# A 4096 x 4096 x 4096 matmul with GELU on one core: A transposed by VectorE from a staged layout, and another opening

## The chip, the cores and the metric

The kernel runs on one core of a Trainium2 chip. The time is the device time of one execution in microseconds (us). A kernel's time is the median of its runs. Beside the times there is one profiled execution with its trace; its span runs from the first to the last recorded instruction.

Names used below: TensorE (PE; its weight loads are PEld), VectorE (DVE), ScalarE (ACT), GpSimd (POOL) and SyncE (SP) are the engines. SBUF is the on-chip memory, PSUM the accumulators of TensorE (eight banks). A load is a DMA that an engine's queue issues; GpSimd's queue issues the loads here, since they convert float32 to bfloat16 on the way, and SyncE's queue issues the stores.

## The reference

```
def setup_inputs():
    m, k, n = 4096, 4096, 4096
    return {
        "a": np.random.randn(m, k).astype(np.float32),
        "b": np.random.randn(k, n).astype(np.float32),
    }

def reference(a: np.ndarray, b: np.ndarray) -> np.ndarray:
    x = np.matmul(a, b)
    return 0.5 * x * (1 + np.tanh(np.sqrt(2 / np.pi) * (x + 0.044715 * x**3)))
```

TensorE multiplies a 128 x 128 piece of A, held with K on the partitions (so A has to be transposed), by a 128 x 512 piece of B, also with K on the partitions. A 128 x 512 result tile sums 32 such matmuls in one PSUM bank. The whole product is 8192 matmuls.

## The kernel before

The rows of A are taken in four blocks of 1024 (`mb`). A block holds eight row tiles of 128 (`ms`), kept transposed in `aT` (one buffer for the whole kernel). For each block all eight chunks of 512 columns of B (`nci`) are loaded as `Bc` (128 x 32 x 512, 4 MB as bfloat16; two buffers), each with one load on GpSimd's queue (L88). For each chunk and row tile, 32 matmuls (L97) run over all of K into one PSUM bank `acc` (four banks). I call the 8 x 32 = 256 matmuls of one chunk in one block a pass.

A is transposed by TensorE. `emit_build` loads a row tile in two halves (L65, 128 partitions x 8 KB of float32 each, stage `a16`, eight buffers), transposes it in 128 x 128 pieces into PSUM (`tp`, L73, two banks), and ScalarE copies four pieces at a time into `aT` (L81). The first block's builds stand in the first pass, before each row tile's matmuls; the build of the next block's row tile stands in a block's last pass, behind the row tile's matmuls.

The result tile goes from PSUM to SBUF (ScalarE, L105), three VectorE instructions compute x(1 + 0.044715 x^2) (L107, L108, L116), ScalarE applies a sigmoid (L117), VectorE multiplies by x (L119), and SyncE's queue stores the tile (L120).

The order of the instructions on each engine is not simply the order of the code. The framework's scheduler hands out the buffers of each pool, puts the instructions of each engine in an order, and adds the waits on semaphores; an instruction whose buffer is free can come ahead of one that stands earlier in the code.

Of the kernel before, what the change touches and what calls it, by code (L numbers as in the profile page):

```python
# [2 lines left out]

# [5 lines left out]

F32 = mybir.dt.float32  # L10
BF16 = mybir.dt.bfloat16
ACT = mybir.ActivationFunctionType
ALU = mybir.AluOpType

GELU_C = 0.044715
SIG_SCALE = 2.0 * math.sqrt(2.0 / math.pi)


@with_exitstack
def kernel(  # L20
    ctx: ExitStack,
    tc: tile.TileContext,
    a: bass.AP,
    b: bass.AP,
    out: bass.AP,
):
    nc = tc.nc
    P = nc.NUM_PARTITIONS

    M, K = a.shape  # L30
    K2, N = b.shape
    assert K == K2
    assert M % P == 0 and K % P == 0 and N % P == 0

    MB = min(1024, M)
    assert M % MB == 0
    NMB = M // MB
    MS_PER = MB // P
    NC = min(512, N)
    assert N % NC == 0  # L40
    NCH = N // NC
    NKT = K // P
    KSTAGE = min(K, 2048)
    assert K % KSTAGE == 0 and KSTAGE % P == 0
    KT_PER_STAGE = KSTAGE // P
    TPG = min(4, KT_PER_STAGE)
    assert KT_PER_STAGE % TPG == 0

    const_pool = ctx.enter_context(tc.tile_pool(name="const", bufs=1))
    at_pool = ctx.enter_context(tc.tile_pool(name="at", bufs=1))  # L50
    astage_pool = ctx.enter_context(tc.tile_pool(name="astage", bufs=8))
    bc_pool = ctx.enter_context(tc.tile_pool(name="bc", bufs=2))
    ev_pool = ctx.enter_context(tc.tile_pool(name="ev", bufs=3))
    psum_pool = ctx.enter_context(tc.tile_pool(name="psum", bufs=4, space=bass.MemoryType.PSUM))

    ident = const_pool.tile([P, P], BF16, name="ident")
    make_identity(nc, ident[:])

    aT = at_pool.tile([P, NKT, MB], BF16, name="aT")

    def emit_build(mb: int, ms: int):
        row0 = mb * MB + ms * P
        for kh in range(K // KSTAGE):
            a16 = astage_pool.tile([P, KSTAGE], BF16, name="a16", tag="a16")
            nc.gpsimd.dma_start(  # L65
                out=a16[:, :],
                in_=a[row0 : row0 + P, kh * KSTAGE : (kh + 1) * KSTAGE],
            )
            for g in range(KT_PER_STAGE // TPG):
                tp = psum_pool.tile([P, TPG * P], BF16, name="tp", tag="tp", bufs=2)  # L70
                for j in range(TPG):
                    ktl = g * TPG + j
                    nc.tensor.transpose(  # L73
                        tp[:, j * P : (j + 1) * P],
                        a16[:, ktl * P : (ktl + 1) * P],
                        ident[:, :],
                    )
                kt0 = kh * KT_PER_STAGE + g * TPG
                src = tp.rearrange("p (j q) -> p j q", j=TPG)
                dst = aT[:, kt0 : kt0 + TPG, ms * P : (ms + 1) * P]  # L80
                nc.scalar.copy(out=dst, in_=src)  # L81

    for mb in range(NMB):
        m0 = mb * MB
        for nci in range(NCH):
            n0 = nci * NC
            Bc = bc_pool.tile([P, NKT, NC], BF16, name="Bc", tag="bc")
            nc.gpsimd.dma_start(  # L88
                out=Bc[:, :, :],
                in_=b[:, n0 : n0 + NC].rearrange("(kt p) n -> p kt n", p=P),  # L90
            )
            for ms in range(MS_PER):
                if mb == 0 and nci == 0:
                    emit_build(0, ms)
                acc = psum_pool.tile([P, NC], F32, name="acc", tag="acc", bufs=4)
                for kt in range(NKT):
                    nc.tensor.matmul(  # L97
                        acc[:, :],
                        aT[:, kt, ms * P : (ms + 1) * P],
                        Bc[:, kt, :],  # L100
                        start=(kt == 0),
                        stop=(kt == NKT - 1),
                    )
                x_sb = ev_pool.tile([P, NC], F32, name="x_sb", tag="x")
                nc.scalar.activation(x_sb[:, :], acc[:, :], ACT.Copy)  # L105
                w = ev_pool.tile([P, NC], F32, name="w", tag="w")
                nc.vector.tensor_tensor(out=w[:, :], in0=x_sb[:, :], in1=x_sb[:, :], op=ALU.mult)  # L107
                nc.vector.tensor_scalar(  # L108
                    out=w[:, :],
                    in0=w[:, :],  # L110
                    scalar1=GELU_C,
                    scalar2=1.0,
                    op0=ALU.mult,
                    op1=ALU.add,
                )
                nc.vector.tensor_tensor(out=w[:, :], in0=w[:, :], in1=x_sb[:, :], op=ALU.mult)  # L116
                nc.scalar.activation(w[:, :], w[:, :], ACT.Sigmoid, scale=SIG_SCALE)  # L117
                y = ev_pool.tile([P, NC], F32, name="y", tag="y")
                nc.vector.tensor_tensor(out=y[:, :], in0=w[:, :], in1=x_sb[:, :], op=ALU.mult)  # L119
                nc.sync.dma_start(  # L120
                    out=out[m0 + ms * P : m0 + (ms + 1) * P, n0 : n0 + NC],
                    in_=y[:, :],
                )
                if nci == NCH - 1 and mb + 1 < NMB:
                    emit_build(mb + 1, ms)


# [1 line left out]
_INS = ['a', 'b']  # L129
_OUTS = [((4096, 4096), 'float32')]  # L130


# [23 lines left out]
```

## Time and profile before

| | |
|---|---|
| median of 3 runs | 1891.46 us (1891.25 to 1892.04) |
| span of the profiled execution | 1889.7 us, granted TensorE clock 1.000 |
| busy: TensorE, VectorE, ScalarE, GpSimd | 1832.4, 655.4, 446.2, 88.8 us |
| HBM read, written | 335.54 MB, 67.11 MB |
| loads on GpSimd's queue | 32 of Bc, 64 of a |
| stores on SyncE's queue | 256 |

A group row of the profile reads: line, engine, operation, output <- input, shapes, count | busy us, mean ns of one | idle time of the engine ahead of them, and what ended it. A row in order of time reads: start, duration (both us), engine, line, operation, names, count, and in brackets the idle time ahead of it with what ended it. A row of the view by stretches reads: start:end, length, busy us and count of PE, PEld, DVE, ACT and POOL, the granted clock, the mean busy share of the 16 DMA engines, and GB/s as landed. Matmuls are pipelined, so the duration of one matmul is longer than the distance from one to the next.

### The profile page before, as it was taken

What the parts mean: (1) busy time and instruction counts of PE and PEld (TensorE: products, weight loads), DVE (VectorE), ACT (ScalarE), POOL (GpSimd) and SP (SyncE); (2) the same over time, 40 slices, a digit from 0 to 9 for tenths busy, and PEclk for the clock granted to TensorE, in tenths of its full rate; (3) what the DMA queues carried; (4) which work ended last, traced back from release to release, by engine and by line L of the source; (5) the groups of instructions that cost most, each with busy time, mean ns of one, the idle gap of its engine ahead of it and who ended that gap; (6) DMA issues with size and microseconds to landing.
All of it is one profiled execution on the core that took longest, in us unless ns stands there. A gap on an engine that the chain in (4) does not pass through costs nothing.

```text
span 1889.7 us, 21528 instructions
## 1 busy us (share of the span) xinstructions
PE 1832.4 (97%) x9033; PEld 860.3 (46%) x9216; DVE 655.4 (35%) x1024; ACT 446.2 (24%) x770; POOL 88.8 (5%) x102
## 2 busy tenths in 40 slices
PE   3999999999999999999999999999999999999998
PEld 2444444444544444444554444444454444444443
DVE  0233333333233333333323333333323333333333
ACT  2521111113511111111441111111154111111111
POOL 2100000000100000000110000000000000000000
PEclk9999999999999999999999999999999999999999
DMA  9995445667876664456995666644496445666511
GB/s 191 222 183 107 97 96 120 127 128 137 175 145 128 128 117 98 94 111 129 177 173 108 122 128 128 129 98 97 98 210 117 86 94 117 128 123 129 114 54 40
DMA packets 177761, 236.29 MB, mean 125 GB/s; under 512 B 5632, under 2 KB 136704, under 8 KB 177664
## 3 DMA queue, kind: packets, MB, share of 16 engines
q0 software_dynamic: 140800, 167.78, 52.9%
q1 hardware_dynamic: 36864, 67.13, 9.9%
q8 instruction: 72, 1.18, 0.2%
q14 instruction: 25, 0.20, 0.0%
HBM read 335.54 MB, written 67.11 MB: 213 GB/s over the span
## 4 chain that ended last, share of the span: by engine, by line
PE 94%; ACT 3%; DMA 1%; issue 1%; DVE 1%; POOL 0%; ACTq 0%; POOLq 0%
PE acc L97 92%; PE tp L73 3%; ACT aT L81 1%; DMA a<-in_a_dram 1%; ACT x_sb L105 1%; DVE w L108 0%; ACT w L117 0%; DVE w L107 0%; DVE w L116 0%; POOL Bc L88 0%; ACT L117 0%; DVE y L119 0%; ACTq L105 0%; POOL ident masks.py:199 0%; POOL ident masks.py:197 0%
## 5 line engine op out<-in xcount | busy, mean ns | idle before, releaser
L97 PE MATMUL acc<-Bc,aT 128*128 128x512 bf16 x8009 | 1790.3, 379 | 9.1
L97 PEld LDWEIGHTS <-aT 128*128 128x128 bf16 x8192 | 798.2, 98 | 931.0 <-issue 0.3
L107 DVE TENSOR_TENSOR w<-x_sb 128x512 f32<-128x512 f32 x256 | 177.3, 692 | 1015.6 <-ACT x_sb L105 1015.6
L105 ACT ACTIVATE x_sb<-acc 128x512 f32<-128x512 f32 x256 | 152.9, 597 | 944.4 <-PE acc L97 915.3
L117 ACT ACTIVATE w<-w 128x512 f32<-128x512 f32 x256 | 161.1, 629 | 465.9 <-DVE w L116 465.9
L119 DVE TENSOR_TENSOR y<-w,x_sb 128x512 f32<-128x512 f32 x256 | 177.1, 692 | 198.2 <-ACT w L117 198.2
L116 DVE TENSOR_TENSOR w<-w,x_sb 128x512 f32<-128x512 f32 x256 | 177.3, 693 | 8.8
L81 ACT COPY aT<-tp 128x512 bf16<-128x512 bf16 x256 | 136.7, 586 | 28.8 <-PE tp L73 28.4
L73 PE MATMUL tp<-ident,a 128*128 128x128 bf16 x1024 | 95.0, 221 | 41.2 <-DMA a<-in_a_dram 28.3
L108 DVE TENSOR_SCALAR w<-w 128x512 f32<-128x512 f32 x256 | 123.7, 483 | 8.7
L88 POOL DMA_DIRECT2D Bc<-in_b_dram x32 | 54.0, 1687 | 1439.3 <-PE acc L97 1398.2
L73 PEld LDWEIGHTS <-a 128*128 128x128 bf16 x1024 | 76.5, 98 | 91.0 <-issue 45.6
L65 POOL DMA_DIRECT2D a<-in_a_dram x64 | 34.2, 537 | 245.6 <-PE tp L73 226.6
L81 ACT ACT_TABLE_LOAD x1 | 1.3, 1283 | 0.7 <-PEq L140 0.7
L117 ACT ACT_TABLE_LOAD x1 | 1.3, 1283 | 0.0
masks.py:199 POOL TENSOR_SCALAR_AFFINE_SELECT ident<-ident 128x128 bf16<-128x128 bf16 x1 | 0.3, 306 | 0.1
masks.py:197 POOL MEMSET ident<- 128x128 bf16 x1 | 0.2, 205 | 0.3 <-POOLq L140 0.3
L140 POOL MEMSET const-float32-0.0<- 128x1 f32 x1 | 0.1, 99 | 0.2 <-issue 0.2
L140 POOL MEMSET const-bfloat16-1.0<- 128x1 bf16 x1 | 0.1, 102 | 0.0
L140 POOL MEMSET const-uint8-127<- 128x1 uint8 x1 | 0.1, 102 | 0.0
L140 POOL MEMSET const-float32-1.0<- 128x1 f32 x1 | 0.1, 99 | 0.0
## 6 DMA issues: line engine op xcount, KB each, us to landing
Bc<-in_b_dram POOLq DMA_DIRECT2D x32, 4096.0 KB, 27.2
out_dram<-y SPq DMA_DIRECT2D x256, 256.0 KB, 3.4
a<-in_a_dram POOLq DMA_DIRECT2D x64, 512.0 KB, 17.3
```

What stands on the lines that cost most here:

```text
L65: nc.gpsimd.dma_start(out=a16[:, :], in_=a[row0 : row0 + P, kh * KSTAGE : (kh + 1) * KSTAGE],)
L73: nc.tensor.transpose(tp[:, j * P : (j + 1) * P], a16[:, ktl * P : (ktl + 1) * P], ident[:, :],)
L81: nc.scalar.copy(out=dst, in_=src)
L88: nc.gpsimd.dma_start(out=Bc[:, :, :], in_=b[:, n0 : n0 + NC].rearrange("(kt p) n -> p kt n", p=P),)
L97: nc.tensor.matmul(acc[:, :], aT[:, kt, ms * P : (ms + 1) * P], Bc[:, kt, :], start=(kt == 0), stop=(kt == NKT - 1),)
L105: nc.scalar.activation(x_sb[:, :], acc[:, :], ACT.Copy)
L107: nc.vector.tensor_tensor(out=w[:, :], in0=x_sb[:, :], in1=x_sb[:, :], op=ALU.mult)
L108: nc.vector.tensor_scalar(out=w[:, :], in0=w[:, :], scalar1=GELU_C, scalar2=1.0, op0=ALU.mult, op1=ALU.add,)
L116: nc.vector.tensor_tensor(out=w[:, :], in0=w[:, :], in1=x_sb[:, :], op=ALU.mult)
L117: nc.scalar.activation(w[:, :], w[:, :], ACT.Sigmoid, scale=SIG_SCALE)
L119: nc.vector.tensor_tensor(out=y[:, :], in0=w[:, :], in1=x_sb[:, :], op=ALU.mult)
L140: nc = _bacc.Bacc("TRN2", target_bir_lowering=False, num_devices=1)
```

## The change

- A's loads. A row tile of 128 rows is loaded in four chunks of 1024 along K, each chunk with four loads of 32 partitions. The stage `a16` holds on partition 32g + mm the 256 values of K of group g for the four rows mm, 32 + mm, 64 + mm and 96 + mm (pieces of 1 KB of float32). That makes 16 loads a row tile, 512 in all.
- The transpose. One VectorE instruction per stage transposes it in 32 x 32 blocks, reading with a step of eight elements and writing eight 128 x 128 pieces of the row tile's `aT`. TensorE's transposes, the identity and ScalarE's copies are gone. `aT` is one tile per row tile, with ten buffers.
- B's order along K. Within each 1024 of K, partition p holds rows 8p to 8p + 7, so that B's order fits A's. `Bc` has three buffers and is loaded in four parts of 1024 rows of K; the first two chunks are loaded in 16 parts each.
- The opening. Four row tiles times two chunks of B accumulate in all eight PSUM banks, with the contraction outermost: the loads come quarter by quarter of K, and all eight tiles take a quarter's matmuls before the next quarter. In the last quarter the eight tiles end one after the other.
- After it, row tiles 4 to 7 take chunks 0 and 1, then chunks 2 to 7 follow for all eight row tiles. Each later block goes through the chunks in the reverse order of the block before, and chunks that are still held are not loaded again.
- GELU is one ScalarE instruction from PSUM to the result tile (`Gelu_apprx_tanh`); VectorE's four instructions are gone.

```
-    aT = at_pool.tile([P, NKT, MB], BF16, name="aT")
-    def emit_build(mb: int, ms: int):
...
-                for j in range(TPG):
-                    ktl = g * TPG + j
-                    nc.tensor.transpose(
-                        tp[:, j * P : (j + 1) * P],
-                        a16[:, ktl * P : (ktl + 1) * P],
-                        ident[:, :],
-                    )
...
-                nc.scalar.copy(out=dst, in_=src)
+    at_pool = ctx.enter_context(tc.tile_pool(name="at", bufs=MS_PER + 2))
+    stage_pool = ctx.enter_context(tc.tile_pool(name="stage", bufs=8))
+    bc_pool = ctx.enter_context(tc.tile_pool(name="bc", bufs=3))
+    y_pool = ctx.enter_context(tc.tile_pool(name="y", bufs=4))
+    psum_pool = ctx.enter_context(tc.tile_pool(name="psum", bufs=8, space=bass.MemoryType.PSUM))
+    a_v = a.rearrange("(t mb mm) (c g r) -> t c g mm mb r", mb=4, mm=Q, g=4, r=RUN)
+    b_v = b.rearrange("(c p j) n -> c p j n", p=P, j=NJ)
+    def load_a(t, c):
+        if c == 0:
+            at[t] = at_pool.tile([P, NKT, P], BF16, name="aT", tag="aT")
+        s = stage_pool.tile([P, 4, RUN], BF16, name="a16", tag="a16")
+        for g in range(4):
+            nc.gpsimd.dma_start(out=s[g * Q : (g + 1) * Q, :, :], in_=a_v[t, c, g])
+        src = s.rearrange("p mb (q j) -> p j mb q", j=NJ)
+        dst = at[t][:, c * NJ : (c + 1) * NJ, :].rearrange("p j (mb q) -> p j mb q", mb=4)
+        nc.vector.transpose(dst, src)
...
+    def load_b(n, c, j0, j1):
+        nc.gpsimd.dma_start(
+            out=bc[n][:, c * NJ + j0 : c * NJ + j1, :],
+            in_=b_v[c, :, j0:j1, n * NC : (n + 1) * NC],
+        )
...
+    def finish(acc, t, n):
+        y = y_pool.tile([P, NC], F32, name="y", tag="y")
+        nc.scalar.activation(y[:, :], acc[:, :], ACT.Gelu_apprx_tanh)
+        nc.sync.dma_start(out=out[t * P : (t + 1) * P, n * NC : (n + 1) * NC], in_=y[:, :])
...
+    for c in range(NCHK):
+        for i in range(H):
+            load_a(i, c)
+            for n in range(2):
+                load_b(n, c, 2 * i, 2 * i + 2)
...
+    for c in range(NCHK - 1):
+        for j in range(NJ):
+            for i in range(H):
+                for n in range(2):
+                    mm(accs[i, n], i, n, c * NJ + j)
...
+    work = [(t, n) for t in range(H, MS_PER) for n in range(2)]
+    order = list(range(NCH))
+    for blk in range(MT // MS_PER):
+        for x, n in enumerate(order):
+            if blk == 0 and n < 2:
+                continue
+            work += [(blk * MS_PER + i, n) for i in range(MS_PER)]
+        order = order[::-1]
+    held = [0, 1]
...
+        if n not in held:
+            need.append(("b", n))
+            held = (held + [n])[-3:]
...
+                for c in range(NCHK):
+                    load_a(x, c)
...
+                for c in range(NCHK):
+                    load_b(x, c, 0, NJ)
+        acc = new_acc()
+        for kt in range(NKT):
+            mm(acc, t, n, kt)
+        finish(acc, t, n)
```

More of the change, by code (lines that the diff above doesn't have):

```diff
@@ L12 @@
 ACT = mybir.ActivationFunctionType
-ALU = mybir.AluOpType
-GELU_C = 0.044715
-SIG_SCALE = 2.0 * math.sqrt(2.0 / math.pi)
+P = 128
+Q = 32
+NC = 512
+KC = 1024
+NJ = KC // P
+RUN = Q * NJ
 @with_exitstack
@@ L27 @@
     nc = tc.nc
-    P = nc.NUM_PARTITIONS
     M, K = a.shape
[L31 to L40, printed above, removed]
-    NCH = N // NC
[L42 to L57, printed above, removed]
@@ L59 @@
-    aT = at_pool.tile([P, NKT, MB], BF16, name="aT")
-    def emit_build(mb: int, ms: int):
[L62 to L67, printed above, removed]
-            )
-            for g in range(KT_PER_STAGE // TPG):
-                tp = psum_pool.tile([P, TPG * P], BF16, name="tp", tag="tp", bufs=2)
-                for j in range(TPG):
-                    ktl = g * TPG + j
-                    nc.tensor.transpose(
-                        tp[:, j * P : (j + 1) * P],
-                        a16[:, ktl * P : (ktl + 1) * P],
-                        ident[:, :],
[L77 to L125, printed above, removed]
@@ new lines @@
+    _, N = b.shape
+    NCHK = K // KC
+    NKT = K // P
+    MT = M // P
+    NCH = N // NC
+    MS_PER = 8
+    H = 4
+    at_pool = ctx.enter_context(tc.tile_pool(name="at", bufs=MS_PER + 2))
[4 more added lines that the diff above has]
+    a_v = a.rearrange("(t mb mm) (c g r) -> t c g mm mb r", mb=4, mm=Q, g=4, r=RUN)
@@ new lines @@
+    b_v = b.rearrange("(c p j) n -> c p j n", p=P, j=NJ)
+    at = {}
+    bc = {}
+    def load_a(t, c):
[7 more added lines that the diff above has]
+        nc.vector.transpose(dst, src)
@@ new lines, in new_b, with mm @@
+    def new_b(n):
+        bc[n] = bc_pool.tile([P, NKT, NC], BF16, name="Bc", tag="bc")
+    def load_b(n, c, j0, j1):
[3 more added lines that the diff above has]
+        )
+    def mm(acc, t, n, kt):
+        nc.tensor.matmul(
+            acc[:, :], at[t][:, kt, :], bc[n][:, kt, :],
+            start=(kt == 0), stop=(kt == NKT - 1),
+        )
+    def finish(acc, t, n):
+        y = y_pool.tile([P, NC], F32, name="y", tag="y")
+        nc.scalar.activation(y[:, :], acc[:, :], ACT.Gelu_apprx_tanh)
+        nc.sync.dma_start(out=out[t * P : (t + 1) * P, n * NC : (n + 1) * NC], in_=y[:, :])
@@ new lines, in new_acc @@
+    def new_acc():
+        return psum_pool.tile([P, NC], F32, name="acc", tag="acc")
+    new_b(0)
+    new_b(1)
+    accs = {}
+    for c in range(NCHK):
[5 more added lines that the diff above has]
+        for n in range(2):
+            accs[i, n] = new_acc()
+    for c in range(NCHK - 1):
+        for j in range(NJ):
+            for i in range(H):
+                for n in range(2):
+                    mm(accs[i, n], i, n, c * NJ + j)
@@ new lines @@
+    c = NCHK - 1
+    for j in range(NJ - 2):
+        for i in range(H):
+            for n in range(2):
+                mm(accs[i, n], i, n, c * NJ + j)
+    for i in range(H):
+        for n in range(2):
+            for j in range(NJ - 2, NJ):
+                mm(accs[i, n], i, n, c * NJ + j)
+            finish(accs[i, n], i, n)
+    work = [(t, n) for t in range(H, MS_PER) for n in range(2)]
[6 more added lines that the diff above has]
+        order = order[::-1]
@@ new lines @@
+    held = [0, 1]
+    plan = []
+    for t, n in work:
+        need = []
+        if t not in at and ("a", t) not in plan:
+            need.append(("a", t))
+            plan.append(("a", t))
+        if n not in held:
+            need.append(("b", n))
+            held = (held + [n])[-3:]
+        yield_loads = need
+        for kind, x in yield_loads:
+            if kind == "a":
+                for c in range(NCHK):
+                    load_a(x, c)
+            else:
+                new_b(x)
+                for c in range(NCHK):
[4 more added lines that the diff above has]
+        finish(acc, t, n)
```

4 lines of the change are left out of this document (1 added, 3 removed).

## The prediction

> **What bounds the kernel now.** I read the page's busy shares, its chain and its costliest groups first, then GpSimd's queue in order of time, then the two ends of the span.
>
> ```profile
> span 1889.7 us, 21528 instructions
> PE 1832.4 (97%) x9033; PEld 860.3 (46%) x9216; DVE 655.4 (35%) x1024; ACT 446.2 (24%) x770; POOL 88.8 (5%) x102
> ...
> PE 94%; ACT 3%; DMA 1%; issue 1%; DVE 1%; POOL 0%; ACTq 0%; POOLq 0%
> ...
> L97 PE MATMUL acc<-Bc,aT 128*128 128x512 bf16 x8009 | 1790.3, 379 | 9.1
> ...
> L73 PE MATMUL tp<-ident,a 128*128 128x128 bf16 x1024 | 95.0, 221 | 41.2 <-DMA a<-in_a_dram 28.3
> ```
>
> TensorE is the chain. Its 379 ns is the length of one pipelined matmul, not its price, and 183 of 8192 records are missing, so I take the price from the spacing of the Bc loads: from the third on, each waits for the pass (256 matmuls) that frees its buffer.
>
> ```profile
> 111.78 1.69 POOL L88 DMA_DIRECT2D Bc<-in_b_dram  x1 [4.65 <-PE acc L97]
> ...
> 388.16 1.69 POOL L88 DMA_DIRECT2D Bc<-in_b_dram  x1 [53.57 <-PE acc L97]
> ...
> 573.31 1.70 POOL L88 DMA_DIRECT2D Bc<-in_b_dram  x1 [52.35 <-PE acc L97]
> ...
> 849.69 1.68 POOL L88 DMA_DIRECT2D Bc<-in_b_dram  x1 [53.56 <-PE acc L97]
> ```
>
> Between 573.31 and 849.69 lie five passes without transposes: 276.38 / 5 = 55.28 us, 215.9 ns a matmul. From 388.16 to 849.69 lies one whole block of eight passes with the next block's 256 transposes: 461.53, against 8 x 55.28 = 442.2. So a block's transposes cost 19.3 us of TensorE. The first pass ends at 111.78; without its 55.28 of matmuls the opening costs 56.5.
>
> ```profile
> 1882.80 0.60 ACT L105 ACTIVATE x_sb<-acc 128x512 f32<-128x512 f32 x1 [3.67 <-PE acc L97]
> ...
> 1886.07 0.69 DVE L119 TENSOR_TENSOR y<-w,x_sb 128x512 f32<-128x512 f32 x1 [0.76 <-ACT w L117]
> ```
>
> The matmuls end at 1882.80, the last y is ready at 1886.76, and 2.9 us of store and closing follow: a tail of 6.9. Sum: 32 x 55.28 = 1769.0, opening 56.5, three block changes 58, tail 6.9, together 1890.4 against the span of 1889.7. The median of the runs is 1891.46, so 1.8 us lie around the span.
>
> **The change part by part.**
>
> *Transposes off TensorE.* All 1024 go. Those of the three block changes were wholly in TensorE's stream: minus 58.0 (both bounds, 57 to 59, from the spacing). The first block's are counted in the opening. The matmuls stay 8192 with the same 128x512 shape and as many weight loads: 1769.0 unchanged.
>
> *The 128 VectorE transposes.* No row has one. The nearest:
>
> ```profile
> L107 DVE TENSOR_TENSOR w<-x_sb 128x512 f32<-128x512 f32 x256 | 177.3, 692 | 1015.6 <-ACT x_sb L105 1015.6
> ...
> L117 ACT ACTIVATE w<-w 128x512 f32<-128x512 f32 x256 | 161.1, 629 | 465.9 <-DVE w L116 465.9
> ...
> L108 DVE TENSOR_SCALAR w<-w 128x512 f32<-128x512 f32 x256 | 123.7, 483 | 8.7
> ```
>
> One handles 1024 elements a partition, so twice a one-input row (0.97 us) to twice a two-input row (1.38); I take 1.1, nearer the one-input form that it is. Four make a row tile, about 4.4 us of VectorE against 13.8 of TensorE for a tile's first two uses; VectorE loses its 1024 GELU instructions, so nothing else is in its way. Cost 0. The cover is gone only at four times that price. By the Trainium skill, page "Vector Engine (DVE) Microarchitecture Reference", section "The reshape front-end and per-opcode configuration", the transpose sustains one element per cycle and lane; no run here shows it yet.
>
> *GELU in one ScalarE pass.* One pass of about 0.63 us (the Sigmoid row) per 6.9 us of matmuls: hidden. At the end only, copy, four VectorE steps and Sigmoid (1882.80 to 1886.76, 3.96 us) become 0.63: minus 3.3.
>
> *DMA traffic.* B chunks are loaded 8 + 3 x 5 = 23 times instead of 32, since three stay across a reversal of the order. Bytes were hidden in the steady part already: 0. But A now comes in 512 loads of 32 partitions (128 pieces of 1 KB each) instead of 64, all on GpSimd's queue together with B.
>
> ```profile
> L88 POOL DMA_DIRECT2D Bc<-in_b_dram x32 | 54.0, 1687 | 1439.3 <-PE acc L97 1398.2
> ...
> L65 POOL DMA_DIRECT2D a<-in_a_dram x64 | 34.2, 537 | 245.6 <-PE tp L73 226.6
> ```
>
> The old A load has 128 pieces and costs 537 ns to issue; Bc with 4096 pieces costs 1687, so the price is about 0.5 plus 0.3 ns a piece. The new A load has 128 pieces again: 0.54. Sixteen make a tile, 8.6 us of queue, below 13.8 (row tiles 4 to 7, each used twice in a row). At a block change six of the eight tiles wait for buffers that come free one per 6.9 us from 48.3 us ahead of the change, and the last is needed 48.3 us behind it: 96.6 us for 6 x 8.6 = 52. Hidden.
>
> *The opening.* Before, TensorE waits for Bc and A, then transposes. After, it works as each quarter of K lands, for four row tiles and two B chunks at once, so the loads set the pace.
>
> ```profile
> 0.00:5.00 5.00, 0.00 (x0) 0.00 (x0) 0.00 (x0) 1.28 (x1) 4.03 (x10) 1.00 0.20 25
> ...
> 32.00:34.00 2.00, 2.00 (x13) 1.36 (x12) 0.00 (x0) 1.47 (x3) 0.00 (x0) 1.00 1.05 211
> ...
> 234.00:236.00 2.00, 2.00 (x11) 0.89 (x10) 0.00 (x0) 0.10 (x1) 0.00 (x0) 1.00 1.24 208
> ```
>
> The last two columns are DMA share and GB/s, in bf16 bytes as they land. At 32 only A moves (4 KB landing per packet), at 234 only B (1 KB). Time per packet is share x 16 x bytes / rate: 326 ns and 97.7 ns, a line of 21.6 ns plus 0.0743 ns a byte, so an A piece of 512 B would take 59.6 ns. One quarter holds 2048 A and 2048 B packets. By bytes alone at 208 GB/s, 3.15 MB take 15.1 us; with an A piece as dear as a B packet, 20.2; by the line and B's share of 1.24, 6.2 + 10.1 = 16.2, which I take as it is fitted to both sizes. Issuing (16 x 0.54 + 8 x 0.6 = 13.4) stays below. Full rate starts at about 4 (the first window moved 0.6 us' worth of data by 5.0, and the identity's instructions ahead are gone). The last quarter lands at 4 + 64.8 + 1 for the completion = 70, and its 64 matmuls take 13.8: done at 83.6. Less 55.3 of work, the opening costs 28.3 instead of 56.5: minus 28.2 (bounds 33 and 12).
>
> ```profile
> 29.96 0.63 PE L97 MATMUL acc<-Bc,aT 128*128 128x512 bf16 x1
> ...
> 42.30 0.38 PE L97 MATMUL acc<-Bc,aT 128*128 128x512 bf16 x1
> ...
> 46.12 0.38 PE L73 MATMUL tp<-ident,a 128*128 128x128 bf16 x4 [1.39 <-ACT aT L81]
> ```
>
> After the long first wait matmuls run slow (0.63) until about 34, with 1.00 granted in every window; after 1.39 us of idleness they are still fast. My gaps between quarters are 2.4 us, so I charge slow matmuls in the first quarter alone, where the next landing hides them. The Trainium skill, page "TensorE: Matmul & The Clock Gate", section "Part 1: The HAM clock gate", puts the fall to half speed after about 3.4 us idle: by that rule with wider gaps each later quarter would lose some 1.7 us more, an estimate, and the sum would be about 5 higher. That both gaps here fit the rule is all the trace shows.
>
> **Sum.** 1889.7 - 58.0 - 3.3 - 28.2 = 1800.2 for the span, plus 1.8 around it: 1802. What is late next is TensorE itself; only the opening and 3.6 of tail are left beside its matmuls.
>
> **The rivals.**
>
> *A chunk late at each reversal.* The three buffers of Bc then hold, say, chunks 5, 6, 7, read in the order 7, 6, 5; chunk 4 can go where 7 was, or, if buffers are handed on by age of loading, has to wait for 5's last reader. Before, both rules give the same order, so its trace can't tell. The price:
>
> ```profile
> DMA to landing us min/median/max: 24.5/27.2/38.0
> ```
>
> (of Bc). Chunk 4's last quarter would land 27.2 after the pass, its last 8 matmuls take 1.7, and 6.9 of that is work: 22.0 lost, three times 66: 1868. For it: the chunk that the code drops from its list is the one loaded first. Against it: the next rival's rows show a load going out ahead of its turn once it has a buffer, so buffers seem to be given by what is free.
>
> *B's third chunk goes ahead of A's last loads.* The queue's order is not the program's:
>
> ```profile
> 3.44 3.77 POOL L65 DMA_DIRECT2D a<-in_a_dram  x7
> 26.11 0.54 POOL L65 DMA_DIRECT2D a<-in_a_dram  x1 [18.91 <-DMA Bc<-in_b_dram]
> ...
> 35.25 1.70 POOL L88 DMA_DIRECT2D Bc<-in_b_dram  x1
> ```
>
> The second Bc went out at 35.25 with five A loads of the first block still to come, though the code puts it behind them. A whole chunk in the midst of the opening costs 4.19 MB / 208 = 20.2: 1822. Against it: there the A loads lacked buffers; here the eight stage buffers come free as fast as quarters land.
>
> *The small A loads are the bound: slower.* The ninth load, at 26.11, sat 18.91 us until the first landed, though its own buffer had never been used: eight loads are in flight, no more. If a small load takes L from issue to landing, the queue yields one per L/8. Landing times of the old A loads were:
>
> ```profile
> DMA to landing us min/median/max: 5.9/17.3/36.4
> ```
>
> At 5.9 that is 0.74 us a load, 11.8 a tile, hidden. At 1.16 us (L = 9.3) the quarters take 16 x 1.16 + 4.8 = 23.4 (plus 28 in all), tiles 4 to 7 wait 4 x 4.8 = 19, and a block change 6 x 18.6 - 96.6 = 15, times three 45: 92, which eats the gain of 89.5. Above it the change loses; at 1.25 (L = 10) plus 130 gives 1932. For it: median and maximum. Against it: these are loads of eight times the bytes, behind a 4 MB chunk. The Trainium skill, page "DMA: Bandwidth & Descriptors", section "Bandwidth", calls transfers under 64 KB dominated by descriptors and asks for 1 MiB each; section "Anatomy of one DMA" gives 2.0 us fixed each, by which 128 KB loads one at a time would be far past 1.16, and eight abreast far below. The row at 26.11 is for the latter.
>
> **How the numbers follow.** The forecast, 1802 with its own range 1793 to 1826 (15.1 to 20.2 us a quarter, slow matmuls or a late start): 0.62. B's chunk ahead, or another loss of that size (1826 to 1855): 0.12. Late chunks at reversals, 1850 to 1885: 0.17. Small loads as the bound: 0.07 slower. Gain and loss cancelling: 0.02. The range 1793 to 1870 holds the first two and over half of the third, 0.84. A measurement tells about 0.2% (4 us) from no change; so faster 0.90, same 0.03, slower 0.07.
>
> **What would show it.** Right: no TensorE transposes; passes still 55.3 us apart across block changes; the last opening matmuls near 84 with gaps of 2 to 3 us between quarters; VectorE transposes near 1.1 us; the end 3.6 us behind the last matmul. Wrong: TensorE idle some 22 us in the fourth pass of blocks 2 to 4 with Bc as releaser; idle stretches ahead of row tiles with a VectorE transpose as releaser, GpSimd waiting on A loads; the opening ending past 100.

## The result: 1800.86 us, against 1802 forecast

The changed kernel takes 1800.86 us (median of 4 runs, 1799.22 to 1802.37) beside 1891.43 of the kernel before on the same chip: a ratio of 0.9521, 95% interval 0.9507 to 0.9534. The profiled run's span is 1798.2. First the profile's page, the rows that answer to those of before (busy shares, chain, groups):

```profile
span 1798.2 us, 18458 instructions
...
PE 1765.6 (98%) x8029; PEld 801.5 (45%) x8192; DVE 248.7 (14%) x128; ACT 153.8 (9%) x257; POOL 371.5 (21%) x632
...
L74 PE MATMUL acc<-Bc,aT 128*128 128x512 bf16 x8029 | 1765.6, 379 | 29.0 <-DMA Bc<-in_b_dram 18.2
...
L62 DVE STREAM_TRANSPOSE aT<-a 128x1024 bf16<-128x1024 bf16 x128 | 248.7, 1983 | 1101.6 <-PE acc L74 965.1
L59 POOL DMA_DIRECT2D a<-in_a_dram x512 | 275.9, 553 | 452.4 <-DVE aT L62 348.1
L81 ACT ACTIVATE y<-acc 128x512 f32<-128x512 f32 x256 | 152.5, 597 | 1640.7 <-PE acc L74 1573.9
```

TensorE has matmuls only, and its whole idle time ahead of them is 29.0 us. VectorE has 128 transposes of 1.98 us, GpSimd's queue 512 loads of A at 0.553. The loads of B in order of time, and the last GELU:

```profile
524.07 3.50 POOL L68 DMA_DIRECT2D Bc<-in_b_dram  x4 [24.61 <-PE acc L74]
...
745.10 3.47 POOL L68 DMA_DIRECT2D Bc<-in_b_dram  x4 [51.80 <-PE acc L74]
...
1187.11 3.47 POOL L68 DMA_DIRECT2D Bc<-in_b_dram  x4 [51.78 <-PE acc L74]
```

```profile
1794.68 0.60 ACT L81 ACTIVATE y<-acc 128x512 f32<-128x512 f32 x1 [6.31 <-PE acc L74]
```

From 745.10 to 1187.11 is one whole block with its change: 442.01, where before it was 461.53. That is eight passes of 55.25 and nothing else. The matmuls end at 1794.68 and the span 3.5 later. So 32 x 55.25 = 1768.0, an opening of 26.7 and the tail of 3.5. Against before: block changes 3 x 19.5 = 58.6, opening 29.8, tail 3.4, together 91.8; the spans differ by 91.5.

### The profile page after: what moved, and what is told of

Its sections match the earlier page's. It is cut to its first block, busy times and chain, and to the rows that moved or that the text cites. A ratio compares the mean times of both kernels' runs of the same rounds, so it can differ in the third digit from the quotient of the medians.

```text
span 1798.2 us, 18458 instructions
## 1 busy us (share of the span) xinstructions
PE 1765.6 (98%) x8029; PEld 801.5 (45%) x8192; DVE 248.7 (14%) x128; ACT 153.8 (9%) x257; POOL 371.5 (21%) x632
## 3 DMA queue, kind: packets, MB, share of 16 engines
q8 instruction: 64, 1.05, 0.2%
## 4 chain that ended last, share of the span: by engine, by line
PE 94%; DMA 3%; POOL 2%; issue 1%; DVE 0%; ACT 0%; DVEq 0%; ACTq 0%; POOLq 0%
PE acc L74 94%; DMA Bc<-in_b_dram 2%; POOL a L59 1%; DMA a<-in_a_dram 1%; POOL Bc L68 0%; DVE aT L62 0%; ACT y L81 0%; DVEq L62 0%; ACTq L81 0%; POOLq L163 0%; POOLq L59 0%
## 5 line engine op out<-in xcount | busy, mean ns | idle before, releaser
L74 PE MATMUL acc<-Bc,aT 128*128 128x512 bf16 x8029 | 1765.6, 379 | 29.0 <-DMA Bc<-in_b_dram 18.2
L62 DVE STREAM_TRANSPOSE aT<-a 128x1024 bf16<-128x1024 bf16 x128 | 248.7, 1983 | 1101.6 <-PE acc L74 965.1
L59 POOL DMA_DIRECT2D a<-in_a_dram x512 | 275.9, 553 | 452.4 <-DVE aT L62 348.1
L81 ACT ACTIVATE y<-acc 128x512 f32<-128x512 f32 x256 | 152.5, 597 | 1640.7 <-PE acc L74 1573.9
L68 POOL DMA_DIRECT2D Bc<-in_b_dram x116 | 96.0, 836 | 808.7 <-PE acc L74 593.5
## 6 DMA issues: line engine op xcount, KB each, us to landing
Bc<-in_b_dram POOLq DMA_DIRECT2D x84, 1024.0 KB, 19.5
```

Of the source, the lines that this page charges most:

```text
L59: nc.gpsimd.dma_start(out=s[g * Q : (g + 1) * Q, :, :], in_=a_v[t, c, g])
L62: nc.vector.transpose(dst, src)
L68: nc.gpsimd.dma_start(out=bc[n][:, c * NJ + j0 : c * NJ + j1, :], in_=b_v[c, :, j0:j1, n * NC : (n + 1) * NC],)
L74: nc.tensor.matmul(acc[:, :], at[t][:, kt, :], bc[n][:, kt, :], start=(kt == 0), stop=(kt == NKT - 1),)
L81: nc.scalar.activation(y[:, :], acc[:, :], ACT.Gelu_apprx_tanh)
```

## The experiments

**What each part is worth.** Two kernels on the way from before to after. The first changes GELU alone:

```
-                x_sb = ev_pool.tile([P, NC], F32, name="x_sb", tag="x")
...
-                nc.vector.tensor_tensor(out=y[:, :], in0=w[:, :], in1=x_sb[:, :], op=ALU.mult)
+                y = ev_pool.tile([P, NC], F32, name="y", tag="y")
+                nc.scalar.activation(y[:, :], acc[:, :], ACT.Gelu_apprx_tanh)
```

> The kernel before with GELU as one ScalarE pass and nothing else changed. Theory: only the tail shrinks, 3.3 us: about 1888. Rival: ScalarE also copies the transposed pieces, and TensorE waited 9.4 us in all for those copies; with less GELU work in the way up to 9 more are gained: about 1879.

Measured: 1887.61 beside 1891.19 (11 runs beside 15; ratio 0.9981, 0.9973 to 0.9990): 3.6 less. The tail gives 3.4 of it (6.9 before, 3.5 in this kernel's profile), so the theory holds. TensorE's waits for ScalarE's copies fell a little as well, from 9.4 to 7.3 us, not by the 9 of the rival.

The second takes the new opening out of the changed kernel:

```
-    new_b(0)
-    new_b(1)
...
-            finish(accs[i, n], i, n)
...
-    work = [(t, n) for t in range(H, MS_PER) for n in range(2)]
+    work = []
...
-            if blk == 0 and n < 2:
-                continue
...
-    held = [0, 1]
+    held = []
```

> The changed kernel without its new opening: row tiles one after the other from the first, each over all of K, loads in that order; VectorE transposes, one-pass GELU and the kept chunks stay. Theory (the new opening is worth what the forecast gave it, about 28 to 31 us against an opening in the old order): the first chunk of B lands near 34, then row tiles 1 to 7 come at the pace of their loads, 16 x 0.55 = 8.8 us or more each against 6.9 of matmuls, the first pass ends near 105, so the time is about 1827 (1820 to 1850, the upper part if another B chunk comes between). Rival (what the old opening lost was its 256 TensorE transposes, 19.3 us, and the order hardly matters): about 1812, no more than 12 above the changed kernel.

Measured: 1831.1 (ratio 0.9681, 0.9668 to 0.9694), 30.2 above the changed kernel. The rival falls: with TensorE's transposes gone the old order still costs about what it did, because the loads set its pace. Its loads of A and the matmuls of the last row tiles of the first pass, in order of time:

```profile
80.17 8.58 POOL L59 DMA_DIRECT2D a<-in_a_dram  x16 [0.49 <-DMA a<-in_a_dram]
...
92.22 5.74 PE L74 MATMUL acc<-Bc,aT 128*128 128x512 bf16 x24 [0.67 <-DVE aT L62]
98.42 1.90 PE L74 MATMUL acc<-Bc,aT 128*128 128x512 bf16 x8 [0.47 <-DVE aT L62]
101.76 1.90 PE L74 MATMUL acc<-Bc,aT 128*128 128x512 bf16 x7 [1.44 <-DVE aT L62]
```

Sixteen loads take 8.6 us of queue where a row tile has 6.9 of matmuls, so TensorE waits for transposes at nearly every tile of the first pass: 13.9 us in all, against 2.2 in the changed kernel, which uses each tile twice. Its waits for loads of B, at the start and at the second chunk, come to 32.7 against 18.2. From before to after the time falls by 3.6 with GELU, by 56.5 from there to the kernel without the new opening (1887.6 to 1831.1), and by 30.2 with the opening. The middle step holds everything else that was changed: the transposes off TensorE, A's new loads and the kept chunks of B.

**The rivals' prices.** Buffers of Bc handed out strictly in turn of loading:

```
-    bc_pool = ctx.enter_context(tc.tile_pool(name="bc", bufs=3))
+    bc_pool = ctx.enter_context(tc.tile_pool(name="bc", bufs=1))
+    taken = []
...
-        bc[n] = bc_pool.tile([P, NKT, NC], BF16, name="Bc", tag="bc")
+        bc[n] = bc_pool.tile([P, NKT, NC], BF16, name="Bc", tag=f"bc{len(taken) % 3}")
+        taken.append(n)
```

> The changed kernel with the three buffers of Bc handed out strictly in turn of loading, so that the first new chunk after a reversal takes the place of the chunk read last. Theory (the forecast's rival, with its price): TensorE waits about 22 us in the fourth pass of blocks 2 to 4, 66 in all: about 1867. Rival (the scheduler or the quarter-wise loading hides it): 1801.

Measured: 1856.08 (ratio 0.9813, 0.9800 to 0.9826), 55.2 above the changed kernel, 18.4 a reversal. TensorE in the fourth pass of the second block, and the same place by stretches (the column ahead of the last two is the granted clock):

```profile
647.46 3.20 PE L76 MATMUL acc<-Bc,aT 128*128 128x512 bf16 x8 [10.36 <-DMA Bc<-in_b_dram]
652.49 2.75 PE L76 MATMUL acc<-Bc,aT 128*128 128x512 bf16 x12 [1.83 <-DMA Bc<-in_b_dram]
657.55 2.97 PE L76 MATMUL acc<-Bc,aT 128*128 128x512 bf16 x13 [2.31 <-DMA Bc<-in_b_dram]
662.61 17.64 PE L76 MATMUL acc<-Bc,aT 128*128 128x512 bf16 x80 [2.09 <-DMA Bc<-in_b_dram]
```

```profile
638.00:640.00 2.00, 0.00 (x0) 0.00 (x0) 0.00 (x0) 0.00 (x0) 2.00 (x3) 0.97 0.59 139
640.00:642.00 2.00, 0.00 (x0) 0.00 (x0) 0.00 (x0) 0.00 (x0) 0.88 (x2) 0.50 0.94 138
```

The mechanism is the rival's: four waits, one per quarter of the chunk, and the half clock after some 3 us of idleness. The size was taken at 22.0: a landing of 27.2 us, with 24 matmuls of one row tile done meanwhile. Here the last quarter's matmuls start at 662.61, 25.5 us after the pass, and 33 matmuls (7.1 us) of this row tile and the next ones are done by then, which leaves 18.4. In the changed kernel itself the load at 524.07 went out at the end of the second block's first pass (a matmul ended its wait), so it took the buffer that was free first, and there are no such waits.

Half as large loads of A:

```
-            nc.gpsimd.dma_start(out=s[g * Q : (g + 1) * Q, :, :], in_=a_v[t, c, g])
+            for h in range(0, Q, 16):
+                nc.gpsimd.dma_start(out=s[g * Q + h : g * Q + h + 16, :, :], in_=a_v[t, c, g, h : h + 16])
```

> The changed kernel with every load of A cut into two of 16 partitions: 32 a row tile, 1024 in all, same bytes and pieces. Theory (each load costs about 0.52 us of GpSimd's queue whatever its size, so 16.6 a row tile against 13.8 of matmuls in the two-chunk stage and 16.1 at a block change): the opening's quarters take 32 x 0.52 + 4.8 = 21.4 instead of 17, row tiles 4 to 7 wait about 3 each, the block changes 1 each: about 1832 (1820 to 1845). Rival (bytes set the pace, not the number of loads): 1801.

Measured: 1853.11 (ratio 0.9792, 0.9777 to 0.9807), 52 above the changed kernel and 8 past the stated upper end. The price of a load was right, the pace was not. The group of loads, and GpSimd's queue through one group of the opening:

```profile
L60 POOL DMA_DIRECT2D a<-in_a_dram x1024 | 514.1, 523 | 583.5 <-DVE aT L63 350.0
```

```profile
30.63 0.51 POOL L60 DMA_DIRECT2D a<-in_a_dram  x1 [0.94 <-DMA Bc<-in_b_dram]
31.13 1.44 POOL L69 DMA_DIRECT2D Bc<-in_b_dram  x2
32.55 3.58 POOL L60 DMA_DIRECT2D a<-in_a_dram  x7
36.83 0.51 POOL L60 DMA_DIRECT2D a<-in_a_dram  x1 [0.70 <-DMA Bc<-in_b_dram]
```

Eight loads of A and two of B take 6.2 us: 5.5 of issuing and 0.7 in which the next load waits for a B in flight, so a quarter takes 25 instead of 21.4. TensorE starves long enough there to lose its clock: granted 0.88 over the stretch from 10 to 110, where the changed kernel had 1.00. At the block changes nothing was lost (no TensorE wait after 201.11). So the forecast's rival of the small loads is real. At 1.05 us of queue for what is now one load of 0.553, more than half of the gain is gone.

**VectorE's transposes.** Two kernels: one reads 32 neighbouring elements (time alone; its sums pair other rows of A and B), one does each transpose twice.

```
-        src = s.rearrange("p mb (q j) -> p j mb q", j=NJ)
+        src = s.rearrange("p mb (j q) -> p j mb q", j=NJ)
```

> The changed kernel with VectorE's transposes reading 32 neighbouring elements at a time instead of every eighth; the sums then pair other rows of A and B, so this is a measurement of time alone. Theory (the 1.98 us against the forecast's 1.1 are the price of reading with a step of eight): the transpose takes about 1.1 us, and the time falls by at most 2 us (the opening). Rival (a 2-byte transpose takes two cycles an element in any order): 1.98 us again and about 1801.

```profile
L62 DVE STREAM_TRANSPOSE aT<-a 128x1024 bf16<-128x1024 bf16 x128 | 154.7, 1232 | 1192.9 <-PE acc L74 992.5
```

Measured: 1.23 us a transpose and 1800.37 (2 runs). Reading every eighth element costs 0.75 of the 1.98, the theory; the time does not move. An element of a partition takes 1.2 ns in the flat read and 1.9 in the read with a step; VectorE's one-input instruction before (L108, 483 ns for 512 elements) takes 0.94. The Trainium skill, page "Vector Engine (DVE) Microarchitecture Reference", section "The reshape front-end and per-opcode configuration", has the transpose sustain one element per cycle and lane. If L108's pace is taken for one element a cycle, the flat read comes near that and the read with a step does not.

```
         nc.vector.transpose(dst, src)
+        nc.vector.transpose(dst, src)
```

> The changed kernel with each VectorE transpose done twice, 4 us a stage and 15.9 a row tile. Theory (VectorE is hidden, with the cover that the forecast named: 13.8 us of matmuls for row tiles 4 to 7, 16.1 a tile at a block change): nothing is lost at the block changes, row tiles 4 to 7 wait 2 each and the opening 2: about 1810 (1803 to 1816). Rival (the spare time is smaller than counted, since loads and transposes of a tile follow one another): 20 or more lost, with waits on VectorE ahead of the first pass of blocks 2 to 4.

Measured: 1814.04 (ratio 0.9594, 0.9579 to 0.9608), 13.2 lost. What TensorE waited for from 120 to the end:

```profile
PE acc L75 <- DVE aT L63: 5.5, 4, 2.0
```

These four waits belong to row tiles 4 to 7, the last of them ahead of 141.98; the rest was lost before 120. The block changes lost nothing, as the theory has it, though a tile then takes 15.9 us of VectorE.

**What sets the opening.** The next five kernels change the opening's loads or the order of its matmuls. First the changed kernel itself: TensorE in order of time, and its queue of loads.

```profile
8.22 0.59 PE L74 MATMUL acc<-Bc,aT 128*128 128x512 bf16 x1 [8.22 <-DMA Bc<-in_b_dram]
...
12.44 16.46 PE L74 MATMUL acc<-Bc,aT 128*128 128x512 bf16 x63 [1.38 <-DMA Bc<-in_b_dram]
...
69.17 4.48 PE L74 MATMUL acc<-Bc,aT 128*128 128x512 bf16 x20 [1.80 <-DMA Bc<-in_b_dram]
74.31 14.40 PE L74 MATMUL acc<-Bc,aT 128*128 128x512 bf16 x65 [0.67 <-DMA Bc<-in_b_dram]
```

```profile
8.57 0.63 POOL L59 DMA_DIRECT2D a<-in_a_dram  x1
9.86 1.62 POOL L59 DMA_DIRECT2D a<-in_a_dram  x3 [0.67 <-DMA Bc<-in_b_dram]
```

In the queue, a wait like the 0.67 here stands in nearly every group of four loads of A and two of B, and a group takes about 4.3 us. TensorE does not wait for whole quarters: it starts at 8.22, on the first part, and some 28 of the opening's 256 matmuls are left at 74.31. The scheduler put the matmuls in the order in which the parts of a quarter land: four are done by 11.06, while in the code's order the third would need the second row tile, which is transposed at 13.36. To see what that is worth, each accumulator's first matmul of a quarter was made to need the part that lands last (the flags for the first and last matmul of a sum go with it):

```
-        for j in range(NJ):
+        for j in reversed(range(NJ)):
...
-            for j in range(NJ - 2, NJ):
+            for j in (1, 0):
```

> The changed kernel with the eight pieces of each quarter of the opening taken in reverse order, so that every accumulator's first matmul of a quarter needs the part that lands last; loads, counts and everything else as they are. Theory (the opening beat the forecast because TensorE works on the parts of a quarter as they land): the last part lands near 76, 64 matmuls of 13.8 follow, the opening's matmuls end near 90 instead of 80: about 1811, up to 4 more if the gaps of some 3.5 us between quarters bring the slow clock. Rival (the order inside a quarter doesn't matter): 1801.

```profile
56.21 0.38 PE L74 MATMUL acc<-Bc,aT 128*128 128x512 bf16 x1 [2.94 <-DMA Bc<-in_b_dram]
...
76.31 53.90 PE L74 MATMUL acc<-Bc,aT 128*128 128x512 bf16 x244 [0.22 <-DMA Bc<-in_b_dram]
```

Measured: 1809.06 (ratio 0.9566, 0.9553 to 0.9579): 8.2 lost, the theory, a little under its 10. TensorE's last wait for the opening's loads ends 2.0 later than in the changed kernel, at 76.31 instead of 74.31, and some 60 matmuls instead of 28 are left then: about 7 us is what the order is worth.

Larger loads of B, in two forms:

```
-            for n in range(2):
-                load_b(n, c, 2 * i, 2 * i + 2)
+            load_b(i % 2, c, 4 * (i // 2), 4 * (i // 2) + 4)
```

> The changed kernel with B's loads of the opening twice as large: per row tile and quarter one load of half a quarter of one chunk instead of two loads of a quarter of a quarter, so 80 loads in the opening instead of 96, same bytes. Theory (the opening goes at the pace of issuing plus the waits that eight loads in flight bring, 4.3 us a group of A and B, not at the DMA rate): a group costs 4 x 0.55 + 0.8 = 3.0 to issue, the bytes take 4.05, so the loads land 16 x 0.25 = 4 us sooner: about 1797. Rival (the DMA engines' rate is the limit): 1801; coarser parts could cost a microsecond.

```
-            for n in range(2):
-                load_b(n, c, 2 * i, 2 * i + 2)
+        for n in range(2):
+            load_b(n, c, 0, NJ)
```

> The changed kernel with, per quarter of the opening, the four row tiles of A first and then each chunk's quarter of B in one load (72 loads). Theory (most of the 2.8 us by which the opening beat the forecast, and more, comes from TensorE working on a quarter's parts as they land, in an order that the scheduler chose): now TensorE can begin a quarter only at its end, as the forecast assumed; the last quarter lands near 66 to 70 and its 64 matmuls take 13.8, so the opening costs about 27 to 30 and the time is about 1802 to 1806. Rival (the order inside a quarter doesn't matter, larger loads do): 1797.

Measured: 1800.86 for the halves (4 runs, 1800.31 to 1805.95; ratio 0.9528, 0.9514 to 0.9542), no gain, and 1812.74 for the quarters (ratio 0.9582, 0.9566 to 0.9598), 12 lost where 1 to 5 were expected. Neither theory held on the loads: larger ones did not land sooner. GpSimd's queue with B by quarters:

```profile
30.00 1.77 POOL L68 DMA_DIRECT2D Bc<-in_b_dram  x2
31.75 3.28 POOL L59 DMA_DIRECT2D a<-in_a_dram  x6
40.32 0.55 POOL L59 DMA_DIRECT2D a<-in_a_dram  x1 [5.29 <-DMA Bc<-in_b_dram]
45.96 4.94 POOL L59 DMA_DIRECT2D a<-in_a_dram  x9 [5.09 <-DMA Bc<-in_b_dram]
```

After two loads of B and six of A the queue stands still until the first B has landed, then again for the second. When that is done the DMA engines have little to do (share 0.78 and 91 GB/s from 46 to 50, against 1.23 and 201 from 38 to 42), and a quarter takes 20 us. With eight loads in flight in order, one large load among small ones holds up the small ones. TensorE's last wait for the opening's loads ends at 84.67 instead of 74.31, and 49 matmuls instead of some 28 are left then: most of the 12 is the queue, the smaller part the coarser pieces that TensorE can begin on.

Mixing the loads, two of A and one of B:

```
+            if between and g % 2 == 1:
+                between(g // 2)
...
-            for n in range(2):
-                load_b(n, c, 2 * i, 2 * i + 2)
+            load_a(i, c, lambda n: load_b(n, c, 2 * i, 2 * i + 2))
```

> The changed kernel with the opening's loads in the order two of A, one of B, two of A, one of B instead of four of A, two of B: same loads, and any eight in flight now hold two or three of B instead of two to four. Theory (a group takes 4.3 us where its bytes would take 3.8 to 4.05, since issuing stands still while eight are in flight with the two of B behind one another): about 4 us less, 1797. Rival (the pace is that of issuing or of the DMA engines): 1801.

Measured: 1800.73 (5 runs; ratio 0.9524, 0.9511 to 0.9537): nothing. With the halves, which saved 16 loads of issuing and gained nothing either, this speaks against issuing and against the order of the eight in flight as the limit. What was left is the DMA engines' price of small pieces, which the last kernel tests with pieces of A twice as long:

```
-KC = 1024
+KC = 2048
...
-    stage_pool = ctx.enter_context(tc.tile_pool(name="stage", bufs=8))
+    stage_pool = ctx.enter_context(tc.tile_pool(name="stage", bufs=4))
...
-                load_b(n, c, 2 * i, 2 * i + 2)
+                load_b(n, c, 4 * i, 4 * i + 4)
```

> The changed kernel with A and B taken in halves of K instead of quarters: A's pieces are 2 KB of float32 instead of 1 KB (1 KB as they land), 256 loads of A instead of 512, four stage buffers of twice the size, and the opening's parts are twice as large. Theory (the opening goes at the pace of the DMA engines, whose busy share of 1.25 to 1.28 there is as high as in the B-only stretches at 208 GB/s, so that a 512 B piece costs about 73 ns instead of the 60 of the forecast's line, and 1 KB pieces cost 98 as B's do): the opening's loads move at about 205 GB/s instead of 184 and land about 7 us sooner, 28 more matmuls (6 us) are left for the end since the parts are larger: about 1800, with the rate as the sign. Rival (issuing or eight loads in flight set the pace, and sizes don't matter to the rate): the rate stays near 184, and the time is about 1806.

The stretch from 10 to 60 (the last two columns are the DMA engines' share and GB/s), of the changed kernel, of the mixed order and of the longer pieces:

```profile
10.00:60.00 50.00, 43.59 (x180) 17.98 (x182) 23.84 (x12) 0.00 (x0) 42.44 (x71) 1.00 1.26 185
```

```profile
10.00:60.00 50.00, 42.53 (x173) 17.36 (x175) 21.94 (x11) 0.00 (x0) 40.87 (x69) 1.00 1.25 181
```

```profile
10.00:60.00 50.00, 41.18 (x162) 16.93 (x166) 25.40 (x7) 0.00 (x0) 22.51 (x37) 1.00 1.24 203
```

The share is the same, the rate is not: 203 with pieces of 1 KB as they land, 185 with 512 B among them. That is the sign that the theory named, and the rival's 184 did not come: the queue of the last kernel is busy for 22.5 of the 50 us instead of 42.4 and waits more on loads in flight, and the data come faster while the DMA engines are no busier. Eight loads in flight then hold more bytes as well; no run separates that from the longer pieces, only the equal share speaks against it. The transposes of the last kernel are twice as long too (3.84 us), and TensorE waits 14.7 us for them, against 2.2. Its time is 1798.14 (5 runs, 1797.57 to 1798.37; ratio 0.9509, 0.9496 to 0.9522), the lowest here. Against the changed kernel that is 2.7 us or 0.15%. The kernel before was itself 0.7 lower beside it (1890.71) and the two intervals of the ratio overlap, so a gain in time is not shown.

## Why the prediction was right, point by point

- *Transposes off TensorE, 58.0.* Right: a block with its change takes 442.01, and the passes on the way stay at 55.25.
- *Fewer loads of B, 0.* Not run alone. In the trace before no wait of TensorE was ended by a load of Bc, which fits.
- *Tail, 3.3.* Right: 3.4 by the profiles, 3.6 by the kernel with GELU alone.
- *VectorE's transposes, 1.1 us, cost 0.* The size was wrong and the cost right. The nearest rows read and wrote neighbouring elements; this instruction reads with a step of eight and takes 1.98, as much as 1.8 times the forecast. It is hidden all the same: even at 4 us a stage only 13 are lost, all before 142. That the cover holds up to four times the price was wrong: 13.8 against 4.4 is 3.1 times, or 3.45 us a transpose, and at 3.97 the waits were there.
- *Issue, 0.54 a load of A.* Right: 0.553. The opening's loads of B take 0.72 instead of 0.6, which changed nothing.
- *The opening, 28.3.* Near in sum (26.7) by two errors against each other, so part of the agreement is luck. A quarter was taken at 16.2; the transposes in the changed kernel follow one another every 4.3 us, four to a quarter, so 17.3, and the last wait for a load ends at 74.31 instead of 70. The term that was too small is A's piece: if B's packet still takes 97.7 ns, a share of 1.26 and 185 GB/s leave about 70 ns for it instead of 59.6, an estimate that has the small packets of the 96 loads in it. The step that failed is "its 64 matmuls take 13.8": the forecast let TensorE begin the last quarter when all of it had landed, but the scheduler's order leaves some 28 matmuls, so the opening's matmuls end near 80 instead of 83.6. Undone by the reversed order, that was worth about 7. Two of the signs of being right did not come for the same reason: the last matmuls near 84, and gaps of 2 to 3 us between quarters, where the longest was 1.80.
- *Slow matmuls in the first quarter alone.* Right for the changed kernel, whose longest gap after the first parts was 1.80 us. The bound was nearer than thought (below).
- *The late chunk at reversals.* Did not happen; forced, it cost 55 instead of 66, since TensorE had 33 matmuls to do meanwhile and not 24, and the landing was 1.7 shorter.
- *B's third chunk ahead of its turn.* Did not happen: the opening's loads went out in the order of the code.
- *Small loads as the bound.* Did not happen at 0.553 a load and a landing of 4.0 us in the median, against the 9.3 where it would have eaten the gain; cutting the loads in two brought more than half of that loss. Eight loads in flight, read from one row of the trace before, fit the queue's waits in the openings shown here.

## What to carry to other kernels

Price TensorE's transposes by the spacing of whole blocks, not by their busy time; moved to an engine with room they cost nothing here, and that room can be counted in advance per tile. An opening that loads can't keep up with is worth reordering so that each loaded piece is used by several accumulators. What sets its pace then is looked for by comparing the rate at equal busy share of the DMA engines: here longer pieces of A raised it, while 16 loads fewer or another mixing of A and B changed nothing. A queue with a fixed number of loads in flight wants loads of like size; making B's four times as large made the opening slower.

## What the runs showed of the hardware that was not expected

The granted clock fell to half after a gap of a length that the forecast charged nothing for (2.4 us). In the profiled execution of the kernel with B in halves, the slowest of its four (1805.95 us), a gap of 2.49 us is followed by slow matmuls; TensorE in order of time, and by stretches:

```profile
34.42 15.67 PE L74 MATMUL acc<-Bc,aT 128*128 128x512 bf16 x64 [2.49 <-DVE aT L62]
```

```profile
34.00:36.00 2.00, 1.58 (x7) 0.75 (x8) 0.36 (x1) 0.00 (x0) 1.00 (x3) 0.91 1.07 150
36.00:38.00 2.00, 2.00 (x6) 0.59 (x4) 1.73 (x1) 0.00 (x0) 1.98 (x4) 0.50 1.24 181
```

Here the clock falls behind the gap, when the matmuls run again. The same shows in the kernel with the reversed order behind the gap of 2.94 us ahead of 56.21: 0.50 from 58 to 62. The Trainium skill, page "TensorE: Matmul & The Clock Gate", section "Part 1: The HAM clock gate", has the clock fall after at least one idle window of about 3.4 us. The traces differ in the length of the gap: 2.49 and 2.94 us were enough, and the 1.80 in the changed kernel was not. Also, the changed kernel's first matmul took 0.59 us (the row at 8.22), where one at full clock takes 0.38, with a granted clock of 1.00 in the view: ahead of its first change that column did not show the slow clock.

In nine of the kernels GpSimd's queue stood still once in the first 85 us for 1.5 to 2.9 us and the profile names nothing that ended the wait (in the changed kernel 1.73 ahead of 65.14). What it waited for was not settled.
